# Splits of w_out, a bias and the sink on other engines and in other places, and the tile order of the output projections

## The chip, the cores and the metric

The kernel runs on one core of a Trainium2 chip. The metric is device time in microseconds (us); the profile names the engines PE (TensorE, matmul), DVE (VectorE), ACT (ScalarE), POOL (GpSimd) and SP (SyncE, which here only issues DMAs).

## The reference

A trunk of two layers over x of 1024 tokens by 1024 features, with 256 memory tokens, all float32; a final RMSNorm stands behind the second layer.

```python
# layer 0
aq, ak, av, bq, bk, bv, xq, gate = split(rmsnorm(x, norm_g) @ w_in)
y_a = windowed_gqa_sink(aq, ak, av, sink, table)   # |i-j| <= 128, bias by distance, 6 heads
y_b = dense_gqa(rope(rmsnorm(bq)), rope(rmsnorm(bk)), bv)          # 6 heads
y_x = memory_cross_attention(xq, mem_n, w_mem_kv)                  # 4 heads
x = x + (concat(y_a, y_b, y_x) * silu(gate)) @ w_out
# layer 1: 6 heads of differential attention (softmax minus lam * softmax) in the place of a and b
# in windowed_gqa_sink, for each head and query:
p = softmax(concat([logits, sink_col], axis=-1), axis=-1)[..., :-1]
```

The sink is one more logit per head, which adds to a softmax's sum and has no value row.

## The kernel before

**Numbers.** Every float32 factor of a matmul is kept as two parts, a rounded high half and the rest as a low half (names: `wh`/`wl` of input weights, `woh`/`wol` of w_out, `yh`/`yl` of the gated head outputs, `PTh`/`PTl` of the transposed probabilities). A product is three matmuls: high by high, high by low, low by high.

**Stages.** Layer 0: the normalised x and its transposes, then attention. Attention is a list of steps, one for a head and 128 queries (dense, "B", and cross-attention, "X") or a head and twice 128 queries (windowed, "A"): 8 of X, 8 of the first B head, and then 40 of B and 24 of A mixed by the pattern `PAT`. `run_steps` writes them out: the scores of step i (PE, `sb` or `sa` in a PSUM buffer of 128x1024, of which there are two), the exponential, the normalisation; a hop of the probabilities through a DMA (`er<-e`, on SP's queue); three steps later (`LAG`) their transposes on PE (`te`, `ta`) and, a step after, the product with the values (`ob`, `oa`). Between these pieces run_steps draws matmuls from a queue of jobs: the projections of heads that come later (`acc`), and when those are done the partial output projection (`pre`, L660), which multiplies the head outputs that are finished by w_out. Nothing of this order is decided at run time: each engine carries out its instructions as the program, after a scheduler, has them, and waits where an operand is missing.

**A dense step.** DVE takes the minimum `mn` of the negated scores (L1059) and multiplies it by the query's norm, `mr` (L1063, 128x1); ACT computes exp with `mr` as bias and the row sums `z` (L1064, 128x1024); DVE the reciprocal `rz` (L1067); POOL multiplies (L1068).

**A windowed step.** For each of its two query blocks DVE adds the distance bias and takes the minimum with the sink (`nsink`, its negative) in one instruction (L1132); ACT computes exp with sums (L1136, 128x384, or 128x256 at the ends of the sequence). Then ACT computes the sink's own exponential `es` (L1139, 128x2), DVE adds it to the sums (L1141) and takes the reciprocal (L1143), POOL multiplies twice (L1149).

**The splits of w_out.** `load_wout` (L248 to L258) loads a piece of 128x512 of w_out by DMA (`wor`), ACT casts it to the high half (L257), and DVE (even pieces) or POOL (odd ones) subtracts for the low half (L258). There are 16 pieces in a layer, two column halves of 8; `wout_hook` calls it from between the steps once the input projections are far enough.

**Output projection.** `out_proj` takes the 8 token tiles in the order `ORD[l]`. A tile is two accumulators of 128x512 (`po`), both halves of one of the two 128x1024 PSUM buffers (`ps_s`); the last tile alone has other buffers (`ps_a`, `ps_t`) and two evictions. `PRE` says which tiles have k-rows behind them from `pre`: in layer 0 the tiles 2 to 5 have 4 of 8 left (24 matmuls), 6 and 7 have 2 left (12), 0 and 1 all 8 (48); in layer 1 the tiles 2, 3 and 4 have 2 left, the others 8. Each tile is then added to x by DVE (L1274), squared and summed by ACT (L1275), normalised (DVE L1283, POOL L229, DVE L1295), and in layer 0 transposed on PE (`tx`, L344) with a split by ACT and DVE (L315, L316) to make layer 1's input `h`. The transposes of a tile stand behind the matmuls of the next one on PE.

Of the kernel before, what the change touches and what calls it, by code (L numbers as in the profile page):

```python
# [13 lines left out]
F32R = mybir.dt.float32r  # L14
# [4 lines left out]
P = 128  # L19
# [13 lines left out]
FAST = ("m0", "m1", "m2", "m3")  # L33
ORD = ((0, 1, 2, 3, 4, 5, 6, 7), (0, 1, 4, 2, 5, 3, 6, 7))
JORD = "xq0 m0 g6 m1 m2 g7 m3 bk bq0 bv bq1 g3 bq2 ak av aq0 g0 aq1 g4 g1 aq2 g5 g2".split()
# [120 lines left out]
def encoder_kernel(ctx, tc, A):  # L156
# [93 lines left out]
    def load_wout(l, i, pl):  # L250
        nh, k = divmod(i, 8)
        if k == 0:
            wtile.append([pl.tile([P, 8, 512], F32R, tag="h", name="wo" + c, bufs=4) for c in "hl"])
        raw = sg(M, "wor", F32) if i % 2 else wp.tile([P, 512], F32, tag="wr", name="wor", bufs=2)
        dma(raw, w_out[l][KORD[l][k], :, nh * 512:(nh + 1) * 512])
        hi, lo = (t[:, k, :] for t in wtile[nh])
        (nc.vector.tensor_copy if WHI[l] else nc.scalar.copy)(hi, raw)  # L257
        (nc.gpsimd if i % 2 else nc.vector).tensor_tensor(out=lo, in0=raw, in1=hi, op=ALU.subtract)  # L258
        return hi, lo
# [8 lines left out]

    wout, wtile, half = {}, [], [0]
    chunks = {}  # L270

# [762 lines left out]
    if True:  # L1034
        def b_step(h, qb):
# [8 lines left out]
            def s1(h=h, qb=qb, e=e):  # L1044
# [17 lines left out]
                mr = stat("mr")  # L1062
                nc.vector.tensor_tensor(out=mr, in0=mn, in1=rq[:, qb, h:h + 1], op=ALU.mult)  # L1063
                nc.scalar.activation(et, Sp, AF.Exp, bias=mr, scale=nrq[:, qb, h:h + 1], accum_out=z)  # L1064
                def finish():
                    rz = stat("rz")
                    nc.vector.reciprocal(rz, z)  # L1067
                    nc.gpsimd.tensor_tensor(out=et, in0=et, in1=rz.to_broadcast([P, 1024]), op=ALU.mult)  # L1068
                    e[0] = et
# [39 lines left out]
    if True:  # L1109
        def a_step(h, p):  # L1110
# [5 lines left out]
            def s1(h=h, p=p, e=e):  # L1116
# [5 lines left out]
                Sp = ps_s("sa").rearrange("p (j c) -> p j c", j=2)  # L1122
                et = new_e(M)[:, :768].rearrange("p (j c) -> p j c", j=2)
                mn = stat("mn2", 2)
                z = stat("z2", 2)
                for j in range(2):
                    qb = 2 * p + j
# [7 lines left out]
                                                   accum_out=mn[:, j:j + 1])  # L1135
                    nc.scalar.activation(et[:, j, c:c + n], et[:, j, c:c + n], AF.Exp,  # L1136
                                         bias=mn[:, j:j + 1], scale=-1.0, accum_out=z[:, j:j + 1])
                es = stat("es", 2)
                nc.scalar.activation(es, mn, AF.Exp, bias=sinkb[:, h:h + 1], scale=1.0)  # L1139
                def finish():  # L1140
                    nc.vector.tensor_tensor(out=z, in0=z, in1=es, op=ALU.add)  # L1141
                    rz = stat("rz2", 2)
                    nc.vector.reciprocal(rz, z)  # L1143
                    for j in range(2):
# [3 lines left out]
                        ej = et[:, j, c:c + hi - lo]  # L1148
                        nc.gpsimd.tensor_tensor(out=ej, in0=ej, in1=rz[:, j:j + 1].to_broadcast([P, hi - lo]), op=ALU.mult)  # L1149
                    e[0] = et  # L1150
# [3 lines left out]
            def hop(p=p, e=e):  # L1154
                t = M.at.tile([P, 1024], F32R, tag="er", name="er", bufs=M.cfg["er"])[:, :768]
                a, b = (P if p == 0 else 0), (768 - P if p == 3 else 768)
                ef = e[0].rearrange("p j c -> p (j c)")
# [51 lines left out]

    run_steps(steps, jobs, hooks0, lambda i: i % 4 != 3)  # L1210
    jobs.drain()
    top_stack.close()
# [3 lines left out]
    def out_proj(l, hT_next, stack):  # L1216
# [12 lines left out]

        def pieces(i):  # L1230
            if i < TT - 1:
                S2 = ps_s("po")
# [355 lines left out]
```

## Time and profile before

| | us |
|---|---|
| median of 3 runs | 1252.83 |
| lowest, highest | 1251.51, 1255.9 |
| profiled execution, its own time | 1255.58 |
| span of the profile | 1253.8 |
| PE busy | 1205.5 (96%) |
| DVE busy | 817.1 (65%) |
| ACT busy | 640.2 (51%) |
| POOL busy | 413.5 (33%) |

The span is what the profile covers of the execution. A matmul's end is modelled, so a busy PE need not be PE at its peak; the idle time is sure. In a row of a timeline or a group, what stands in brackets or behind the last bar is the idle time of that engine just before, and the instruction that ended it. "issue" is time in which the engine waited for nothing that the profile shows.

### The profile page before, as it was taken

The numbers are of one execution on the slowest core, as the hardware profiler recorded it, in microseconds if no ns is written. First come the engines' busy times: TensorE is split into PE (matmuls) and PEld (weight loads), VectorE is DVE, ScalarE is ACT, GpSimd is POOL, SyncE is SP. The second block draws the span as 40 slices with busy tenths as digits, with TensorE's granted clock in tenths as the row PEclk, the third lists the DMA queues.
The fourth block names the chain that finished last, engine by engine and source line by source line (L and its number), as shares of the span: only waits on it lengthen the run. The fifth ranks groups of instructions, "written<-read, shape, count | busy, mean of one in ns | idle before, by whom it ended". The sixth has DMA issues, their size and how long they took to land. (4 is left out here: it accounts for less than half of the span.)

```text
span 1253.8 us, 19637 instructions
## 1 busy us (share of the span) xinstructions
PE 1205.5 (96%) x6806; PEld 999.2 (80%) x6806; DVE 817.1 (65%) x1545; ACT 640.2 (51%) x1395; POOL 413.5 (33%) x390
## 2 busy tenths in 40 slices
PE   5999999999998999998999999999999999999997
PEld 4887788888887787887888778788887878877876
DVE  5547666377778788746355865766667666678444
ACT  6249654256666766533157644444444454456322
POOL 5023456266666565403122212212122131223100
PEclk9999999999999999999999999999999999999999
DMA  6654444545365575466644334243342433445363
GB/s 252 198 187 149 155 168 150 171 155 201 148 224 191 210 246 186 154 203 213 185 163 144 125 107 120 93 143 108 105 137 76 136 115 118 144 151 189 129 211 118
DMA packets 96350, 199.90 MB, mean 159 GB/s; under 512 B 11478, under 2 KB 31190, under 8 KB 96252
## 3 DMA queue, kind: packets, MB, share of 16 engines
q1 hardware_dynamic: 96252, 198.65, 47.4%
q8 instruction: 54, 0.88, 0.3%
q14 instruction: 44, 0.36, 0.1%
HBM read 79.32 MB, written 31.47 MB: 88 GB/s over the span
## 5 line engine op out<-in xcount | busy, mean ns | idle before, releaser
L297 PE MATMUL acc<-h,wh 128*128 128x512 f32 x1536 | 499.1, 399 | 7.3 <-DVE yt L624 3.1
L297 PEld LDWEIGHTS acc<-h,wh 128*128 128x128 f32 x1536 | 283.2, 188 | 73.3 <-issue 13.4
L297 PE MATMUL acc<-h,wl 128*128 128x512 f32 x768 | 304.6, 397 | 1.8 <-POOL wl L241 1.8
L241 POOL TENSOR_TENSOR wl<-wr,wh 128x512 fp32r<-128x512 f32 x96 | 124.9, 1302 | 340.0 <-DVE wh L239 125.2
L316 DVE TENSOR_TENSOR PTl<-te,PTh 128x512 fp32r<-128x512 f32 x224 | 148.2, 687 | 131.2 <-ACT PTh L315 128.4
L1440 ACT ACTIVATE e<-e,mn 128x1024 f32<-128x1024 f32 x96 | 110.2, 1149 | 130.7 <-DVE mn L1437 127.5
L297 PEld LDWEIGHTS acc<-h,wl 128*128 128x128 f32 x768 | 144.8, 189 | 35.5 <-issue 4.4
L315 ACT CAST PTh<-te 128x512 fp32r<-128x512 f32 x224 | 124.9, 591 | 30.2 <-PE te L540 24.6
L1068 POOL TENSOR_TENSOR e<-e,rz 128x1024 f32<-128x1024 f32 x48 | 91.7, 1913 | 78.1 <-DVE rz L1067 66.7
L1437 DVE CUSTOM_DVE_ANT_0 e<-sc,toep 128x1024 f32<-128x1024 f32 x96 | 113.9, 1217 | 5.3 <-PE sc L1431 5.0
L540 PEld LDWEIGHTS te<-identr,er 128*128 128x128 f32 x896 | 91.8, 143 | 21.1 <-issue 4.1
L540 PE MATMUL te<-identr,er 128*128 128x128 f32 x896 | 100.0, 246 | 7.5 <-issue 3.2
L239 DVE CAST wh<-wr 128x512 fp32r<-128x512 f32 x112 | 59.1, 530 | 43.9 <-PE acc L297 14.4
L1064 ACT ACTIVATE e<-sb,mr,nrq 128x1024 f32<-128x1024 f32 x48 | 58.0, 1208 | 48.4 <-DVE mr L1063 33.9
L1449 DVE SCALAR_TENSOR_TENSOR e<-e,mr 128x1024 f32<-128x1024 f32 x48 | 76.2, 1588 | 1.3
L1464 PE MATMUL oc<-PTh,v 128*128 128x256 f32 x384 | 74.8, 288 | 0.3 <-DVE ckl L1333 0.3
L660 PE MATMUL po<-woh,yh 128*128 128x512 f32 (+1 forms) x172 | 65.9, 383 | 1.5 <-DVE x L1274 1.5
L660 PE MATMUL po<-woh,yl 128*128 128x512 f32 (+1 forms) x172 | 65.6, 381 | 0.0
L660 PE MATMUL po<-wol,yh 128*128 128x512 f32 (+1 forms) x172 | 65.5, 381 | 0.0
L1464 PEld LDWEIGHTS oc<-PTh,v 128*128 128x128 f32 x384 | 61.5, 192 | 0.7 <-DVE ckl L1333 0.6
L1059 DVE TENSOR_REDUCE mn<-sb 128x1 f32<-128x1024 f32 x48 | 58.4, 1216 | 5.1 <-PE sb L509 4.7
L318 ACT ACTIVATE yh<-yr 128x256 fp32r<-128x256 f32 (+2 forms) x56 | 24.0, 448 | 67.3 <-DMA yr<-ysc 38.5
(199 smaller groups left out, 2247.1 us busy)
## 6 DMA issues: line engine op xcount, KB each, us to landing
er<-e SPq DMA_DIRECT2D x112, 512.0 KB, 2.9
wr<-in_w_in SPq DMA_DIRECT2D x96, 256.0 KB, 2.8
ysc<-gy SPq DMA_DIRECT2D x16, 512.0 KB, 2.9
wor<-in_w_out SPq DMA_DIRECT2D x32, 256.0 KB, 3.5
cq<-sg SPq DMA_DIRECT2D x64, 128.0 KB, 2.6
ck<-sg SPq DMA_DIRECT2D x48, 128.0 KB, 2.3
er<-e SPq DMA_DIRECT2D x12, 384.0 KB, 2.8
xpsc<-xh SPq DMA_DIRECT2D x18, 256.0 KB, 2.5
```

Of the source, the lines that this page charges most:

```text
L239: nc.vector.tensor_copy(hi, raw)
L241: (nc.vector if fast else nc.gpsimd).tensor_tensor(out=lo, in0=raw, in1=hi, op=ALU.subtract)
L297: lastmm[0] = nc.tensor.matmul(acc, a, b[:, k, c0:c0 + n], start=(i == 0), stop=(i == 23))
L315: nc.scalar.copy(hi, src)
L316: return nc.vector.tensor_tensor(out=lo, in0=src, in1=hi, op=ALU.subtract)
L540: nc.tensor.transpose(to[:, i * P:(i + 1) * P], e[0][:, k * P:(k + 1) * P], idt)
L660: lastmm[0] = nc.tensor.matmul(acc, a, b, start=(start and n == 0), stop=(stop and n == 2))
L1068: nc.gpsimd.tensor_tensor(out=et, in0=et, in1=rz.to_broadcast([P, 1024]), op=ALU.mult)
L1437: nc.vector.tensor_tensor_reduce(out=et, in0=Sp, in1=toeps[h][:, w0:w0 + 1024], scale=1.0, scalar=BIG, op0=ALU.add, op1=ALU.min, accum_out ...
L1440: nc.scalar.activation(et, et, AF.Exp, bias=mn[:, m:m + 1], scale=-1.0, accum_out=z[:, m:m + 1])
L1449: nc.vector.scalar_tensor_tensor(out=es[0], in0=es[1], scalar=c, in1=es[0], op0=ALU.mult, op1=ALU.add)
L1464: nc.tensor.matmul(acc, V[:, kt, v, :], pt[:, kt, :], start=(n == 0), stop=(n == 23))
```

## The change

Four parts.

1. *Splits of w_out in layer 0.* All 16 low halves go to POOL. Each has a fixed place in the order of its engine: the cast of a high half behind the exponential that was written last (`behind["exp"]`), the low half behind the normalisation written last (`behind["sub"]`). `issue_after` orders two instructions of an engine, and waits for nothing else. Layer 1's splits stay as they were.
2. *mr on ACT.* The product of minimum and norm is an ACT instruction (Identity with a scale), directly ahead of the exponential or with another ACT instruction between.
3. *The sink as a score column.* The windowed step's tile gets a further column behind each block's scores, into which ACT copies the negated sink; exp runs one column wider and its sum then holds the sink. `es` and the addition to z are gone. The rows of the hop are a column longer.
4. *Output projections.* The order of the tiles is (0, 1, 2, 6, 3, 7, 4, 5) in layer 0, where it was 0 to 7, and (0, 1, 5, 2, 6, 3, 4, 7) in layer 1, where it was (0, 1, 4, 2, 5, 3, 6, 7). In both the third tile takes two buffers of `ps_a`, which the projections and `pre` used, and is evicted in two halves.

The number of PE's instructions stays. DVE has 48 `mr`, 24 additions to z and 8 subtractions less, and 2 additions and the halved third tiles more; ACT has 48 `mr` and 30 copies of the sink more, and 24 `es` less; POOL has 8 subtractions more.

```diff
--- before.py
+++ after.py
@@ -31,7 +31,7 @@
 CUTS = ((0, 4, 6, 8), (0, 4, 6, 7, 8))
 LAG = 3
 FAST = ("m0", "m1", "m2", "m3")
-ORD = ((0, 1, 2, 3, 4, 5, 6, 7), (0, 1, 4, 2, 5, 3, 6, 7))
+ORD = ((0, 1, 2, 6, 3, 7, 4, 5), (0, 1, 5, 2, 6, 3, 4, 7))
 JORD = "xq0 m0 g6 m1 m2 g7 m3 bk bq0 bv bq1 g3 bq2 ak av aq0 g0 aq1 g4 g1 aq2 g5 g2".split()
 NB0 = 1
 PAT = "BBABBABBABBABBAA" * 4
@@ -254,8 +254,11 @@
         raw = sg(M, "wor", F32) if i % 2 else wp.tile([P, 512], F32, tag="wr", name="wor", bufs=2)
         dma(raw, w_out[l][KORD[l][k], :, nh * 512:(nh + 1) * 512])
         hi, lo = (t[:, k, :] for t in wtile[nh])
-        (nc.vector.tensor_copy if WHI[l] else nc.scalar.copy)(hi, raw)
-        (nc.gpsimd if i % 2 else nc.vector).tensor_tensor(out=lo, in0=raw, in1=hi, op=ALU.subtract)
+        own = l == 0 and behind["sub"] is not None
+        with (tc.issue_after(behind["exp"].ins) if own else nullcontext()):
+            (nc.vector.tensor_copy if WHI[l] else nc.scalar.copy)(hi, raw)
+        with (tc.issue_after(behind["sub"].ins) if own else nullcontext()):
+            (nc.gpsimd if own or i % 2 else nc.vector).tensor_tensor(out=lo, in0=raw, in1=hi, op=ALU.subtract)
         return hi, lo
 
     def wout_hook(l, jobs, last, pl):
@@ -267,6 +270,7 @@
                 wout[len(wout)] = load_wout(l, len(wout), pl)
 
     wout, wtile, half = {}, [], [0]
+    behind = {"exp": None, "sub": None}
     chunks = {}
 
     def half_done(n=1):
@@ -1060,12 +1064,13 @@
                 et = new_e(M)
                 z = stat("z")
                 mr = stat("mr")
-                nc.vector.tensor_tensor(out=mr, in0=mn, in1=rq[:, qb, h:h + 1], op=ALU.mult)
-                nc.scalar.activation(et, Sp, AF.Exp, bias=mr, scale=nrq[:, qb, h:h + 1], accum_out=z)
+                nc.scalar.activation(mr, mn, AF.Identity, scale=rq[:, qb, h:h + 1])
+                behind["exp"] = nc.scalar.activation(et, Sp, AF.Exp, bias=mr, scale=nrq[:, qb, h:h + 1], accum_out=z)
                 def finish():
                     rz = stat("rz")
                     nc.vector.reciprocal(rz, z)
-                    nc.gpsimd.tensor_tensor(out=et, in0=et, in1=rz.to_broadcast([P, 1024]), op=ALU.mult)
+                    behind["sub"] = nc.gpsimd.tensor_tensor(out=et, in0=et, in1=rz.to_broadcast([P, 1024]),
+                                                            op=ALU.mult)
                     e[0] = et
                 return finish
             st.s1 = s1
@@ -1120,9 +1125,15 @@
                     jobs.ensure("aq%d" % ((h + 1) // 2))
                     load_q(Aq, aq_d, h + 1)
                 Sp = ps_s("sa").rearrange("p (j c) -> p j c", j=2)
-                et = new_e(M)[:, :768].rearrange("p (j c) -> p j c", j=2)
+                et = new_e(M)[:, :770].rearrange("p (j c) -> p j c", j=2)
                 mn = stat("mn2", 2)
                 z = stat("z2", 2)
+                ends = [(min(8, qb + 2) - qb + 1) * P for qb in (2 * p, 2 * p + 1)]
+                if ends[0] == ends[1]:
+                    nc.scalar.copy(et[:, :, ends[0]], nsink[:, h:h + 1].to_broadcast([P, 2]))
+                else:
+                    for j in range(2):
+                        nc.scalar.copy(et[:, j, ends[j]:ends[j] + 1], nsink[:, h:h + 1])
                 for j in range(2):
                     qb = 2 * p + j
                     lo, hi = max(0, qb - 1) * P, min(8, qb + 2) * P
@@ -1133,12 +1144,9 @@
                                                    in1=abias[h][:, c:c + n], scale=1.0,
                                                    scalar=nsink[:, h:h + 1], op0=ALU.add, op1=ALU.min,
                                                    accum_out=mn[:, j:j + 1])
-                    nc.scalar.activation(et[:, j, c:c + n], et[:, j, c:c + n], AF.Exp,
-                                         bias=mn[:, j:j + 1], scale=-1.0, accum_out=z[:, j:j + 1])
-                es = stat("es", 2)
-                nc.scalar.activation(es, mn, AF.Exp, bias=sinkb[:, h:h + 1], scale=1.0)
+                    behind["exp"] = nc.scalar.activation(et[:, j, c:c + n + 1], et[:, j, c:c + n + 1], AF.Exp,
+                                                         bias=mn[:, j:j + 1], scale=-1.0, accum_out=z[:, j:j + 1])
                 def finish():
-                    nc.vector.tensor_tensor(out=z, in0=z, in1=es, op=ALU.add)
                     rz = stat("rz2", 2)
                     nc.vector.reciprocal(rz, z)
                     for j in range(2):
@@ -1146,14 +1154,15 @@
                         lo, hi = max(0, qb - 1) * P, min(8, qb + 2) * P
                         c = lo - (qb - 1) * P
                         ej = et[:, j, c:c + hi - lo]
-                        nc.gpsimd.tensor_tensor(out=ej, in0=ej, in1=rz[:, j:j + 1].to_broadcast([P, hi - lo]), op=ALU.mult)
+                        behind["sub"] = nc.gpsimd.tensor_tensor(
+                            out=ej, in0=ej, in1=rz[:, j:j + 1].to_broadcast([P, hi - lo]), op=ALU.mult)
                     e[0] = et
                 return finish
             st.s1 = s1
 
             def hop(p=p, e=e):
-                t = M.at.tile([P, 1024], F32R, tag="er", name="er", bufs=M.cfg["er"])[:, :768]
-                a, b = (P if p == 0 else 0), (768 - P if p == 3 else 768)
+                t = M.at.tile([P, 1024], F32R, tag="er", name="er", bufs=M.cfg["er"])[:, :770]
+                a, b = (P if p == 0 else 0), (769 - P if p == 3 else 769)
                 ef = e[0].rearrange("p j c -> p (j c)")
                 dma(t[:, a:b].bitcast(F32), ef[:, a:b])
                 e[0] = t.rearrange("p (j c) -> p j c", j=2)
@@ -1208,6 +1217,7 @@
             wout_hook(0, jobs, "g2", r1)
 
     run_steps(steps, jobs, hooks0, lambda i: i % 4 != 3)
+    behind["sub"] = None
     jobs.drain()
     top_stack.close()
     att.close()
@@ -1228,6 +1238,9 @@
             return xr
 
         def pieces(i):
+            if i == 2:
+                p = [(ps_a("po")[:, 0:512], c, 512) for c in (0, 512)]
+                return p, p
             if i < TT - 1:
                 S2 = ps_s("po")
                 return [(S2[:, 0:512], 0, 512), (S2[:, 512:1024], 512, 512)], [(S2, 0, 1024)]
```

Where the first column half of w_out is split, on ACT (`woh` is a high half, `e,z` an exponential with its sum, `PTh` and `PTa` casts of transposed probabilities, `gy` and `yt` head outputs), before:

```order
L1139 ACTIVATE es<-mn_4468,small 128x2
L425 ACTIVATE gy<-acc 128x512
L437 COPY yt<-oa 64x256
L315 CAST PTa<-ta 128x3x128
L315 CAST PTa<-ta 128x2x128
L257 CAST woh<-wor 128x512 x5
L437 COPY yt<-oa 64x256
L1064 ACTIVATE e,z<-sb,mr,nrq 128x1024
L315 CAST PTh<-te 128x4x128 x2
L257 CAST woh<-wor 128x512 x2
```

and now:

```order
L319 CAST PTa<-ta 128x2x128
L1067 ACTIVATE mr<-mn,rq 128x1
L1068 ACTIVATE e,z<-sb,mr,nrq 128x1024
L259 CAST woh<-wor 128x512
L441 COPY yt<-oa 64x256
L319 CAST PTh<-te 128x4x128 x2
L259 CAST woh<-wor 128x512
L1067 ACTIVATE mr<-mn,rq 128x1
L1068 ACTIVATE e,z<-sb,mr,nrq 128x1024
L259 CAST woh<-wor 128x512
```

Before, five casts stand in a row ahead of an exponential and two behind its neighbours; now one or two stand behind each exponential, and `mr` ahead of it.

On POOL, where the first and the second column half are split (`wol` is a low half, L1068 and L1149 the normalisations), before:

```order
L1149 TENSOR_TENSOR e<-e,rz_4517 128x384
L439 TENSOR_TENSOR gy<-yt,gy 64x256
L258 TENSOR_TENSOR wol<-wor,woh 128x512 x3
L439 TENSOR_TENSOR gy<-yt,gy 64x256
L1068 TENSOR_TENSOR e<-e,rz 128x1024
L258 TENSOR_TENSOR wol<-wor,woh 128x512
L1068 TENSOR_TENSOR e<-e,rz 128x1024
L1149 TENSOR_TENSOR e<-e,rz_4701 128x384 x2
L439 TENSOR_TENSOR gy<-yt,gy 64x256
```

and now, a few steps later in the program, where most subtractions come together (lines have moved by 3 to 8: L261 was L258, L1072 was L1068, L1157 was L1149, L443 was L439):

```order
L1072 TENSOR_TENSOR e<-e,rz 128x1024
L261 TENSOR_TENSOR wol<-wor,woh 128x512
L443 TENSOR_TENSOR gy<-yt,gy 64x256
L261 TENSOR_TENSOR wol<-wor,woh 128x512
L1072 TENSOR_TENSOR e<-e,rz 128x1024
L261 TENSOR_TENSOR wol<-wor,woh 128x512 x3
L1157 TENSOR_TENSOR e<-e,rz_5049 128x384
L1157 TENSOR_TENSOR e<-e,rz_5049 128x256
L443 TENSOR_TENSOR gy<-yt,gy 64x256
L1072 TENSOR_TENSOR e<-e,rz 128x1024
L261 TENSOR_TENSOR wol<-wor,woh 128x512 x2
```

Before, POOL has three subtractions together, with none between the two dense normalisations behind them but one; now one to three stand behind nearly every normalisation.

## The prediction

> **What bounds the kernel now.** The page's first table and its chain of waits put PE ahead of all other engines, so a change is worth what it takes out of PE's idle time, or puts in.
>
> ```profile
> span 1253.8 us, 19637 instructions
> PE 1205.5 (96%) x6806; PEld 999.2 (80%) x6806; DVE 817.1 (65%) x1545; ACT 640.2 (51%) x1395; POOL 413.5 (33%) x390
> PE 39%; DVE 2%; issue 2%; ACT 1%; DMA 1%; POOL 0%; POOLq 0%; DVEq 0%; ACTq 0%
> ```
>
> PE is idle for 1253.8 - 1205.5 = 48.3 us. The view of stretches says where. Its columns are the stretch, its length, then busy us and instructions of each engine, and PE's granted clock.
>
> ```profile
> 220.00:375.00 155.00, 153.69 (x922) 131.93 (x921) 103.87 (x234) 87.63 (x191) 87.53 (x77) 1.00 0.53 180
> 375.00:530.00 155.00, 145.57 (x903) 123.13 (x901) 123.24 (x269) 103.66 (x233) 88.47 (x83) 0.99 0.56 199
> 550.00:605.00 55.00, 50.97 (x254) 41.42 (x253) 36.02 (x55) 20.99 (x42) 13.19 (x16) 1.00 0.69 215
> 1200.00:1254.00 54.00, 45.84 (x223) 38.17 (x221) 26.51 (x46) 15.50 (x35) 5.08 (x8) 0.97 0.48 163
> ```
>
> The two first are attention of layer 0, equally long. Without the splits of w_out PE idles 155 - 153.69 = 1.3 us; from 375 on, where the splits and the partial output projections (pre) stand, 155 - 145.57 = 9.4 us. DVE rises from 67% to 80% there, POOL only from 56% to 57%. The third stretch is layer 0's output projection (4.0 us idle), the fourth layer 1's, whose last idle stretch is the kernel's end. PE's waits in the second stretch:
>
> ```profile
> PE te L540 <- issue: 3.2, 5, 1.4
> PE sa L509 <- ACT e L1064: 2.1, 2, 1.1
> PE sa L509 <- DVE mn L1132: 1.3, 2, 1.1
> PE pre L660 <- DVE yt L438: 1.2, 1, 1.2
> ```
>
> The columns are total us, times, longest. What stands behind them is read in the timelines of the four engines (start, duration, engine, operation, idle time before and its releaser):
>
> ```profile
> 393.68 3.78 POOL L258 TENSOR_TENSOR wol<-wor,woh 128x512 fp32r<-128x512 f32 x3
> 394.38 3.64 DVE L258 TENSOR_TENSOR wol<-wor,woh 128x512 fp32r<-128x512 f32 x1
> 397.94 0.15 DVE L1063 TENSOR_TENSOR mr<-mn,rq 128x1 f32<-128x1 f32 x1
> 398.12 1.21 ACT L1064 ACTIVATE e<-sb,mr,nrq 128x1024 f32<-128x1024 f32 x1 [2.48 <-DVE mr L1063]
> 399.47 0.44 PE L509 MATMUL sa<-ak,q 128*128 128x384 f32 x1 [0.98 <-ACT e L1064]
> 401.43 0.50 PE L540 MATMUL te<-identr,er 128*128 128x128 f32 x4 [1.35 <-issue]
> 401.64 1.27 POOL L258 TENSOR_TENSOR wol<-wor,woh 128x512 fp32r<-128x512 f32 x1
> 401.85 1.08 DVE L1063 TENSOR_TENSOR mr<-mn,rq 128x1 f32<-128x1 f32 x1
> 405.35 0.44 PE L509 MATMUL sa<-ak,q 128*128 128x384 f32 x1 [1.07 <-DVE mn L1132]
> 427.01 0.62 ACT L257 CAST woh<-wor 128x512 fp32r<-128x512 f32 x1 [3.38 <-DMA wor<-in_w_out]
> 428.88 0.44 PE L509 MATMUL sa<-ak,q 128*128 128x384 f32 x1 [1.08 <-ACT e L1064]
> 430.65 0.50 PE L660 MATMUL pre<-woh,yh 128*128 128x512 f32 x1 [1.16 <-DVE yt L438]
> ```
>
> Read it as two chains. At 394.38 DVE begins a low half while POOL runs three of them, and is done only as POOL is; mr, the exponential's bias, is queued behind it, ACT stands 2.48 us, and PE waits three times: 0.98 + 1.35 + 1.07 = 3.40 us. At 427.01 ACT's cast of a high half had stood 3.38 us for its load, with the next exponential behind it: 1.08 + 1.16 = 2.24 us on PE. Together 5.64 of the 9.4 us.
>
> **The change, part by part.** Durations of what moves (groups of the whole run: count, busy us, mean ns; or count and min/median/max):
>
> ```profile
> L258 DVE TENSOR_TENSOR wol<-wor,woh 128x512 fp32r<-128x512 f32 x16 | 14.7, 918 | 3.5 <-ACT woh L257 3.5
> L258 POOL TENSOR_TENSOR wol<-wor,woh x8: 1274/1291/1297, 393.7 to 442.5; 128x512 fp32r<-128x512 f32 x8
> L1063 DVE TENSOR_TENSOR mr<-mn,rq 128x1 f32<-128x1 f32 x48 | 9.3, 193 | 0.7
> L1141 DVE TENSOR_TENSOR z<-z,es x24: 148/161/1109, 252.9 to 520.6; 128x2 f32<-128x2 f32 x24
> L1139 ACT ACTIVATE es<-mn,small x24: 278/280/292, 252.5 to 520.3; 128x2 f32<-128x2 f32 x24
> L1483 ACT ACTIVATE z<-ssqc,es 128x1 f32<-128x1 f32 x48 | 10.0, 258 | 4.5 <-PE ssqc L1479 4.3
> ```
>
> *Bias and sink, outside the splits.* The 48 mr leave DVE (9.3 us) for ACT, which ran none; the nearest row is another 128x1 ACTIVATE with a pointer operand, 258 ns, so ACT gets 12.4 us. The 24 es (280 ns, 6.7 us) and the 24 additions to z (161 ns) go; 30 copies of the sink into a score column come. ACT's copies of such a size are not in the trace; between nothing and the 280 ns of es they cost 0 to 8.4 us, and I take 200 ns (nearest: 258, less a pointer), 6.0 us, so they pay for es. The copies wait for no score, so they may run early. In 220 to 375 PE idles only 1.3 us: what could be gained there is at most that, and with ACT at 57% in this stretch what is added has 67 us of ACT idle to go into. A step's exponential starts 258 - 154 = 0.1 us later on its chain, which LAG (three steps between scores and transposes) covers; if that cover were gone, 48 x 0.1 = 5 us at most. I take 0, ends -1.3 and +1.7 (a third of those 5).
>
> *The splits.* Eight low halves leave DVE, at 0.69 (an undisturbed one) to 3.64 us each, and eight come to POOL at 1.29 each: +10.3 us on POOL's 88.5, 64% of the stretch. Each now stands behind a normalisation and so cannot be issued three deep ahead of a step's own; each high half stands behind the exponential that it stood ahead of. The first chain (3.40 us) rests on a DVE subtraction and a DVE mr that are both no longer there; the second (2.24) on a cast ahead of an exponential. Both go: -5.6. The remaining 3.8 us are small waits that I leave. The half clock that followed the second chain
>
> ```profile
> 431.20:434.60 3.40, 3.40 (x15) 2.80 (x14) 2.87 (x7) 2.59 (x6) 1.76 (x2) 0.50 0.69 233
> ```
>
> cost 3.40 x 0.5 = 1.7 us; no row says whether it returns after another stall, so I take half, -0.85. The low bound is all of the excess and the clock: 8.1 + 1.7 = 9.8 us. What waits on POOL's new work is the next normalisation, then its hop through DMA, then te; the hop's row (transfers, KB, median us from issue to landing):
>
> ```profile
> er<-e SPq DMA_DIRECT2D x112, 512.0 KB, 2.9
> ```
>
> These 2.9 us must still fit after a later normalisation. I take +0.5, ends 0 and the 10.3 us of rival 1. Sum of this part: -6.
>
> The Trainium skill speaks on the first chain in SBUF — State Buffer, section "Who interferes with whom": a DVE instruction with two SBUF inputs blocks against a GpSimd instruction that reads SBUF, each for the other's whole length. The 3.64 and the 1.08 us rows agree, and by that rule more subtractions on POOL block whatever such DVE work is left; that would take up to 10.3 us from DVE's relief. On the half clock, TensorE: Matmul & The Clock Gate ("What's actually happening") has a free-running window of 3413 ns that lowers the clock after an idle window; the 3.40 us row has its length, and by the rule the whole 1.7 us returns with the stall, 0.85 less than my sum.
>
> *Output projection of layer 0.* PE's four waits there:
>
> ```profile
> PE tx L344 <- DVE h L316: 1.7, 1, 1.7
> PE tx L344 <- DVE xs L1295: 1.2, 2, 0.7
> PE acc L297 <- DVE v L1283: 1.1, 1, 1.1
> ```
>
> The tiles 6 and 7 (12 matmuls left, against 24 of the tiles 2 to 5) move between longer ones. That gives the last tiles more matmuls to hide a normalisation under (the 1.1 and part of the 1.7 should go, about -2.3), but behind a short tile the transposes of the one before come early. One matmul of this kind takes the distance between two starts:
>
> ```profile
> 1200.17 0.39 PE L660 MATMUL po<-wol,yh 128*128 128x512 f32 x1
> 1200.40 0.39 PE L660 MATMUL po<-woh,yl 128*128 128x512 f32 x1
> ```
>
> so 12 fewer are 12 x 0.23 = 2.8 us less cover. I work out two new waits of about 0.9, so -0.5; ends -4.0 (all waits go) and +3.2 (both new ones as long as the longest here, 1.7, and nothing saved but 0.2).
>
> *Layer 1's end.* The third tile now takes two other PSUM buffers and need not wait for tile 0's to be emptied:
>
> ```profile
> PE po L660 <- DVE x L1274: 1.5, 1, 1.5
> ```
>
> -1.5; ends -1.5 and 0 (the other buffers not free either: they last held partial sums finished well before). The work after the last matmul stays.
>
> **Sum**, against the profiled execution: 0 - 6 - 0.5 - 1.5 = -8.0 us. That execution took 1255.6 us (span 1253.8), 2.7 above the median 1252.8 of the three runs and at their upper end, which no row explains; I carry the difference over to the median: **1244.8, say 1245 us**. All low ends give -1.3 - 9.8 - 4.0 - 1.5 = -16.6, 1236 us.
>
> **Rivals.**
> 1. *POOL becomes the late engine* (slower). Three subtractions still stand in a row in one place and two in another, 1.29 us each, ahead of a step's normalisation. If each of the eight added ones delays its step's te by its whole length, PE idles 8 x 1.29 = 10.3 us more, and by the blocking seen at 401.85 (1.08 us for a 0.15 us instruction) DVE's own work pays too, so that the chains' 5.6 do not come back: +10.3 - 0.5 - 1.5 = +8.3, 1261 us. It decides from the point where more than half of a subtraction shows on PE. For it: te waits already head the list of PE's waits (3.2 us). Against: POOL has 155 - 88.5 = 66.5 us idle in this stretch.
> 2. *Nothing gained among the splits.* ACT, 67% busy there, gets mr, copies and waits at mr for the maximum as it did at the exponential; or the small waits take the place of the long ones. Then the tail and projection alone: -2.0, 1250.8. For it: the waits are spread over five tiles and five releasers. Against: the two chains' owners are taken away outright.
> 3. *The short tiles expose the transposes*: +3.2 in the place of -0.5, 1244.8 + 3.7 = 1248.5. For it: DVE's xs and h are the releasers of every wait there.
> 4. *The fixed places make w_out late*: the last low half stands about one step later, and a partial projection must wait for it. The price is a step, counted by the dense steps' normalisations in this stretch:
>
> ```profile
> L1068 POOL TENSOR_TENSOR e<-e,rz x20: 1887/1893/2266, 383.3 to 512.4; 128x1024 f32<-128x1024 f32 x20
> ```
>
> With half as many windowed steps beside these 20, a step is 130 / 30 = 4.3 us: 1249.1. Against: no PE wait for wol is in the list of waits, so there is room.
>
> **How the numbers follow.** Forecast 0.62 (its own range 1239 to 1249); rival 1 0.12; rival 2 0.13; rival 3 0.08; rival 4 0.05. Faster or slower by over 0.3% (3.8 us, about what this measurement can tell) means below 1249.0 or above 1256.6. The forecast is faster, with half of rival 3 and a few hundredths of the rest: 0.68; the same has rivals 2 and 4 and the other half of 3, 0.20; slower is rival 1, 0.12. The range 1237 to 1255 leaves out rival 1 and the last of the low side.
>
> **What would show it.** In the stretch of the splits PE's idle time falls from 9.4 to about 4 us; no DVE instruction there lasts over 2 us; no exponential stands 2 us for mr or behind a cast; DVE falls to some 110 us, POOL rises to near 99. PE's clock in that stretch tells the half-clock term. In 550 to 605 idle time stays near 4 us with other tiles' names in it; in the tail "po <- DVE x" is gone. I am wrong if te's waits grow and end on POOL's normalisations (rival 1), if PE's idle time among the splits stays above 8 us (rival 2), if tx waits sum to over 6 us (rival 3), or if pre waits for wol (rival 4).

## The result and the profile after

The changed kernel took 1246.9 us (median of 6 runs, 1245.4 to 1247.6) against 1254.4 for the kernel before (6 runs): ratio 0.9938, 95% interval 0.9924 to 0.9953, or 7.8 us less. Timed again later beside other kernels, it was 1249.3 against 1253.4: ratio 0.9961 (0.9948 to 0.9974), 4.9 us less. So it is faster, by 5 to 8 us. Part of the distance between the two timings is PE's granted clock, whose mean was 0.9973 in the first and 0.9953 in the second. Compared within its kernel, over the 160 runs of these experiments, a run was 0.56 us longer for each us that its clock withheld (one minus the clock, times the span). By that estimate the clock makes some 1.4 of the 2.4 us between the timings; where it matters below, differences are also given with the clock taken out in this way.

The page of the kernel after, its span and first table:

```profile
span 1245.0 us, 19673 instructions
PE 1201.2 (96%) x6806; PEld 998.5 (80%) x6806; DVE 801.6 (64%) x1471; ACT 652.1 (52%) x1453; POOL 422.1 (34%) x398
```

PE is still the bound. DVE lost 15.5 us, ACT gained 11.9 and POOL 8.6. The same four stretches as in the prediction, of the kernel after (the last reaches 9 us beyond its end):

```profile
220.00:375.00 155.00, 154.41 (x942) 134.04 (x941) 105.12 (x212) 94.05 (x222) 92.57 (x83) 1.00 0.54 187
375.00:530.00 155.00, 145.13 (x901) 123.56 (x900) 109.00 (x223) 106.13 (x249) 96.73 (x88) 0.99 0.55 197
550.00:605.00 55.00, 52.29 (x257) 42.50 (x256) 36.35 (x59) 20.10 (x41) 12.71 (x15) 1.00 0.71 224
1200.00:1254.00 54.00, 38.75 (x194) 32.89 (x192) 23.12 (x42) 12.28 (x32) 4.24 (x8) 0.96 0.42 148
```

The surprise stands in the second row. DVE fell from 123 to 109 us there, as predicted, and PE is idle for 155 - 145.13 = 9.9 us, where it was 9.4. PE's waits in that stretch:

```profile
PE oa L1196 <- ACT PTa L319: 2.0, 1, 2.0
PE te L544 <- issue: 2.0, 3, 1.5
PE sa L513 <- DVE mn L1143: 2.0, 2, 1.1
PE te L544 <- PE sa L513: 1.5, 2, 0.8
PE sa L513 <- ACT e L1068: 0.9, 1, 0.9
```

Behind the longest of them stands a chain like the prediction's second: a cast of a high half waits for its load, an exponential and the cast PTa stand behind it, and PE waits for PTa (ACT, then PE):

```profile
431.11 0.62 ACT L259 CAST woh<-wor 128x512 fp32r<-128x512 f32 x1 [2.17 <-DMA wor<-in_w_out]
431.64 0.51 ACT L1147 ACTIVATE e<-e,mn 128x257 f32<-128x257 f32 x1
433.16 0.86 ACT L319 CAST PTa<-ta 128x384 fp32r<-128x384 f32 x2
434.07 0.39 PE L1196 MATMUL oa<-PTa,av 128*128 128x256 f32 x1 [2.05 <-ACT PTa L319]
```

Stretches of fixed time hold other work once something ahead moves. So the traces are compared at places of the program: the first dense scores of layer 0, the 48th of the 96 windowed-score matmuls (about where the splits begin), the first matmul of the output projection, the first and last scores of layer 1, the end. Each number is the change of a piece's length against the kernel before, in us of one profiled execution; under "cut windows" stands how often PE's clock was halved for 3.4 us (1.7 us each), ahead of the first dense scores and among the splits.

| kernel | to first scores | attention, no splits | splits | projection, start of layer 1 | layer 1 | end | cut windows |
|---|---|---|---|---|---|---|---|
| before (length) | 142.1 | 234.1 | 154.5 | 158.7 | 470.5 | 93.9 | 1, 1 |
| after | -2.1 | -2.8 | -1.1 | -1.0 | +0.4 | -2.2 | 0, 1 |
| after, again | -2.1 | -3.0 | -0.6 | -0.8 | -0.6 | -2.2 | 0, 1 |
| splits alone | -0.7 | -0.1 | +4.7 | -0.8 | -1.6 | 0.0 | 1, 1 |
| mr alone | -2.3 | -1.8 | -1.0 | -0.2 | +0.6 | 0.0 | 0, 1 |
| sink alone | -2.6 | -0.5 | +0.1 | 0.0 | -0.2 | 0.0 | 0, 0 |
| projections alone | -0.6 | -0.1 | -0.6 | -0.3 | +1.0 | -2.2 | 1, 1 |
| all but splits | -0.6 | -2.9 | +0.9 | -1.5 | 0.0 | -2.2 | 1, 2 |
| all but mr | -2.2 | -0.4 | +2.4 | -1.9 | -0.2 | -2.3 | 0, 2 |
| all but sink | -2.3 | -1.8 | -1.5 | -0.5 | -1.1 | -2.3 | 0, 2 |
| mr on DVE, scalar form | -0.6 | -1.3 | -2.5 | -0.9 | -0.1 | -2.2 | 1, 0 |
| even low halves on DVE | -0.5 | -3.0 | +0.7 | -1.1 | -0.1 | -2.2 | 1, 2 |
| own buffer | -0.9 | -2.8 | +0.8 | -1.4 | -0.5 | -2.2 | 1, 3 |
| own buffer, cast moved | -1.9 | -2.9 | -0.2 | -1.3 | -0.1 | -2.2 | 0, 2 |

The column "to first scores" is no gain of the change: it falls into two groups that go with the cut windows there, and the kernel with the projections alone, whose program is still the one before at that place, and the kernel before differ by 0.6 in it. The columns "projection" and "layer 1" scatter by over 1 us among kernels that are the same there. What the change brings lies in the columns "attention, no splits" and "end". The column "splits" has to be read with the cut windows among the splits: without the splits part it shows +0.9 with two windows, and less the 1.7 us of the second one -0.8, which is what the whole change shows with one (-1.1 and -0.6).

### The profile page after: what moved, and what is told of

Its sections match the earlier page's. It is cut to its first block, busy times and chain, and to the rows that moved or that the text cites. A ratio compares the mean times of both kernels' runs of the same rounds, so it can differ in the third digit from the quotient of the medians.

```text
span 1245.0 us, 19673 instructions
## 1 busy us (share of the span) xinstructions
PE 1201.2 (96%) x6806; PEld 998.5 (80%) x6806; DVE 801.6 (64%) x1471; ACT 652.1 (52%) x1453; POOL 422.1 (34%) x398
## 5 line engine op out<-in xcount | busy, mean ns | idle before, releaser
L1072 POOL TENSOR_TENSOR e<-e,rz 128x1024 f32<-128x1024 f32 x48 | 91.1, 1901 | 77.1 <-DVE rz L1071 58.0
L1068 ACT ACTIVATE e<-sb,mr,nrq 128x1024 f32<-128x1024 f32 x48 | 57.9, 1207 | 2.1
```

The source lines that it names most:

```text
L1072: behind["sub"] = nc.gpsimd.tensor_tensor(out=et, in0=et, in1=rz.to_broadcast([P, 1024]), op=ALU.mult)
```

## The experiments

Four kernels hold one part each, three lack one part each, one puts mr on DVE in another form, and three alter the splits of the changed kernel. Each was timed in 5 to 12 executions.

### Each part alone

**Splits alone** (fixed places, all low halves of layer 0 on POOL):

```diff
-        (nc.gpsimd if i % 2 else nc.vector).tensor_tensor(out=lo, in0=raw, in1=hi, op=ALU.subtract)
+        with (tc.issue_after(behind["sub"].ins) if own else nullcontext()):
+            (nc.gpsimd if own or i % 2 else nc.vector).tensor_tensor(out=lo, in0=raw, in1=hi, op=ALU.subtract)
...
```

> Only the splits of w_out in layer 0 are changed (all low halves on POOL, both halves in fixed places). Theory 1, the prediction's sum: this part is worth most, -6 us against the kernel before, and PE's idle time among the splits falls from 9.4 to about 4 us. Theory 2, from the trace after (PE idles 9.9 us there, the long waits have come back in other places: a cast of a high half that waits 2.17 us for its load, a yh cast that waits 2.86 us, both ahead of an exponential): this part is worth -1 us at most, 0 within what can be told.

Measured: 1257.1 us, ratio 1.0028 (1.0017 to 1.0039), 3.5 us slower. Neither theory had this. Two rows of its timelines (POOL, then DVE) show it:

```profile
448.22 1.90 POOL L1072 TENSOR_TENSOR e<-e,rz 128x1024 f32<-128x1024 f32 x1
448.28 1.85 DVE L1145 TENSOR_TENSOR z<-z,es 128x2 f32<-128x2 f32 x1
```

and the instructions of two lines in it (min/median/max):

```profile
L1067 DVE TENSOR_TENSOR mr<-mn,rq x48: 141/159/1368, 143.8 to 514.0; 128x1 f32<-128x1 f32 x48
L1145 DVE TENSOR_TENSOR z<-z,es x24: 148/163/1848, 252.1 to 524.5; 128x2 f32<-128x2 f32 x24
```

An addition of 128x2 that takes 0.16 us otherwise took 1.85, and ended as POOL's normalisation did. mr took up to 1.37. Not one mr or addition that began while POOL was idle took over 0.17 us, here or in the kernel before; the long ones all began while POOL was at work, and some that did were short all the same. More work on POOL means that such an instruction meets it more often: 12 of the 48 mr began under POOL here, and 6 before.

**mr alone** on ACT:

```diff
-                nc.vector.tensor_tensor(out=mr, in0=mn, in1=rq[:, qb, h:h + 1], op=ALU.mult)
+                nc.scalar.activation(mr, mn, AF.Identity, scale=rq[:, qb, h:h + 1])
```

> Only mr (128x1) moves from DVE to ACT. Theory 1, the sum: 0 (-1.3 to +1.7). Theory 2, from the two traces, where the change gains 2.8 us between the first dense scores and the first partial output projection's stretch, of which mr and the sink column are the only parts: -2 us, and DVE's relief shows in all of layer 0's attention, where 40 steps lose a DVE instruction that stood between the minimum and the exponential.

Measured: 1250.1 us, ratio 0.9975 (0.9964 to 0.9986), 3.1 us faster. Theory 2 had the sign and about the size: 1.8 us of it lie in the attention ahead of the splits, where PE had 1.3 us of plain idle time in the stretch from 220 to 375.

**Sink column alone**:

```diff
-                es = stat("es", 2)
-                nc.scalar.activation(es, mn, AF.Exp, bias=sinkb[:, h:h + 1], scale=1.0)
...
-                    nc.vector.tensor_tensor(out=z, in0=z, in1=es, op=ALU.add)
+                nc.scalar.copy(et[:, :, ends[0]], nsink[:, h:h + 1].to_broadcast([P, 2]))
...
```

> Only the sink becomes a score column (es on ACT and the addition on DVE go, copies on ACT come). Theory 1: 0. Theory 2: a windowed step loses a DVE instruction and a wait between ACT and DVE ahead of its reciprocal, -1 us over 24 steps; if mr brings the whole 2.8 us of the attention before the splits, 0.

Measured: 1255.0 us, ratio 1.0007 (0.9994 to 1.0019): no difference that can be told. The marks give -0.5 us ahead of the splits.

**Output projections alone**:

```diff
-ORD = ((0, 1, 2, 3, 4, 5, 6, 7), (0, 1, 4, 2, 5, 3, 6, 7))
+ORD = ((0, 1, 2, 6, 3, 7, 4, 5), (0, 1, 5, 2, 6, 3, 4, 7))
...
+            if i == 2:
+                p = [(ps_a("po")[:, 0:512], c, 512) for c in (0, 512)]
+                return p, p
```

> Only the output projections change (order of the tiles, third tile in two other buffers). Theory 1, the sum: -0.5 in layer 0 and -1.5 in layer 1, together -2. Theory 2, from the two traces: the marks of PE gain 1.0 us between the first po of layer 0 and the first scores of layer 1, and 2.2 us from the last scores of layer 1 to the end: -3.2. This run also shows whether the 2.1 us that the trace after is ahead by at the first dense scores, where the two programs do not yet differ, comes and goes by itself: its program is the one before up to the output projection.

Measured: 1251.8 us, ratio 0.9985 (0.9974 to 0.9995), 1.9 us faster, -2 expected by the one and -3.2 by the other. The end gains 2.2 to 2.3 us in every kernel that has this part, and 0.0 in the three that lack it; layer 0's projection changes by -0.3 here. (The +1.0 in layer 1 of this run holds a cut window at 722 us, worth 1.7.)

The four ratios add to 3.5 - 3.1 + 0.9 - 1.9 = -0.6 us, each sure to some 1.4 us. The whole gives -4.9 to -7.8. The parts hang together.

### One part taken from the whole

Theory L says why: a DVE instruction that reads two tensors from SBUF can stand still while POOL works, and mr, the addition to z and the even low halves are such instructions. Its rival M: the splits do not matter, the sum fails between mr and the sink column.

**All but the splits:**

```diff
-        own = l == 0 and behind["sub"] is not None
-        with (tc.issue_after(behind["exp"].ins) if own else nullcontext()):
...
+        (nc.gpsimd if i % 2 else nc.vector).tensor_tensor(out=lo, in0=raw, in1=hi, op=ALU.subtract)
```

> The whole change but the splits (mr on ACT, sink column, output projections). The four parts alone gave +3.5, -3.1, +0.9 and -1.9 us by their ratios, which add to -0.6, where the whole gives -7.8. Theory L: a DVE instruction with two SBUF inputs stands still while POOL works; subtractions on POOL hurt only while mr and the addition to z are on DVE, and with both gone they bring the prediction's gain. Then this kernel is near the sum of the other three, -4 us (1250), 3 to 4 us slower than the whole change. Theory M: what does not add is mr with the sink column, and the splits are worth nothing: this kernel is as fast as the whole change (1246 to 1247).

Measured: 1248.8, ratio 0.9973 (0.9959 to 0.9987), 3.4 us faster than before, which is L's -4. Against the whole it is 1.5 us slower by the second timing of the whole (0.9961) and 4.4 by the first (0.9938); with the second the intervals overlap. With the clock taken out this kernel is 5.4 us faster than the one before, and the whole in its second timing 5.7. So a gain from the splits in this company is not shown, and M's price for them, nothing, stands. That they no longer cost 3.5 us is shown. M's reason falls: mr, sink column and projections alone add to -4.1 us, near the -3.4 of the three together, so it is the splits that do not add.

**All but mr** (mr on DVE, as before):

```diff
-                nc.scalar.activation(mr, mn, AF.Identity, scale=rq[:, qb, h:h + 1])
+                nc.vector.tensor_tensor(out=mr, in0=mn, in1=rq[:, qb, h:h + 1], op=ALU.mult)
```

> The whole change but mr, which is back on DVE. Theory L: mr is blocked by the 16 subtractions and the normalisations on POOL (in the splits alone its mean was 359 ns, against 240 before and about 150 undisturbed), so most of the gain is lost: 1252 to 1255. Theory M: the splits do not matter, and mr's own 3.1 us are lost: about 1250.

Measured: 1251.4, ratio 0.9991 (0.9980 to 1.0002). Of the gain 3.8 (second timing) to 6.6 us (first) are lost; the time lies between L's range (1252 to 1255) and M's 1250.

**All but the sink column:**

```diff
-                    behind["exp"] = nc.scalar.activation(et[:, j, c:c + n + 1], et[:, j, c:c + n + 1], AF.Exp,
+                    behind["exp"] = nc.scalar.activation(et[:, j, c:c + n], et[:, j, c:c + n], AF.Exp,
...
+                    nc.vector.tensor_tensor(out=z, in0=z, in1=es, op=ALU.add)
```

> The whole change but the sink column: es and the addition to z are back. Theory L: the addition (two SBUF inputs, 483 ns mean among the splits alone, against 246 before) is blocked, with the minimum of the next windowed block behind it: 2 to 3 us slower than the whole change, about 1249.5. Theory M or any in which only mr matters: as fast as the whole change, since the sink column alone gave nothing.

Measured: 1246.7, ratio 0.9960 (0.9946 to 0.9974): that of the whole's second timing, and 2.8 us slower than its first. L's price of 2 to 3 us is not shown, though the longest addition took 2.15 us in this kernel. The other three parts alone add to -1.5 us here, and to +2.5 without mr, where -5.0 and -1.1 were measured. By these sums, sure to some 2.5 us, either mr or the addition off DVE takes most of the splits' cost away. Why one is enough stays open.

**mr on DVE with one tensor input**, and otherwise the whole change:

```diff
-                nc.scalar.activation(mr, mn, AF.Identity, scale=rq[:, qb, h:h + 1])
+                nc.vector.tensor_scalar(out=mr, in0=mn, scalar1=rq[:, qb, h:h + 1], scalar2=None, op0=ALU.mult)
```

> The whole change, but mr is on DVE in a form with one tensor from SBUF and a 128x1 scalar operand. Theory L: an instruction of one SBUF stream is not blocked (the 128x1 reciprocals, which read one, took 160 ns in every run), so mr takes 150 to 200 ns and the time is that of the whole change, 1246 to 1247, or a little better, as ACT loses 48 instructions of 300 ns. Theory Q: what costs is any DVE instruction between the minimum and the exponential, whatever its inputs, since it queues behind other work: as slow as with mr back on DVE (1250 to 1255).

Measured: 1248.2, ratio 0.9962 (0.9949 to 0.9975): as fast as the second timing of the whole, with mr on ACT, and 3.6 us faster than with mr on DVE as a product of two tensors, with intervals that do not meet. With the clock taken out 2.2 of the 3.6 us are left. Both kernels have mr on the same engine, between the same instructions; only the operand's form differs. All 48 mr of the two kernels (first the two-tensor form):

```profile
L1067 DVE TENSOR_TENSOR mr<-mn,rq x48: 140/159/1364, 142.3 to 510.3; 128x1 f32<-128x1 f32 x48
```

```profile
L1067 DVE TENSOR_SCALAR mr<-mn,rq x48: 189/211/217, 143.9 to 505.8; 128x1 f32<-128x1 f32 x48
```

The scalar form is slower at its median and never over 217 ns, though 14 of the 48 began while POOL was at work; of the two-tensor form 13 did, and 10 of those took over 200 ns. So theory Q, that any DVE instruction in this place costs as much as the two-tensor one, falls. Whether the scalar form gives all that ACT gives is open: in the attention ahead of the splits the marks show -1.3 us with it, -0.4 with the two-tensor form and -2.8 to -3.0 with mr on ACT.

The Trainium skill has the rule, in SBUF — State Buffer, section "Who interferes with whom": a DVE instruction with two SBUF inputs contends with a GpSimd instruction that reads SBUF, and the loser blocks. These rows agree. The page counts `tensor_scalar` among the operations that can contend as well, under conditions; at 128x1 float32 with a 128x1 scalar none of the 48 did.

### What is left among the splits

**Even low halves back on DVE**, odd ones on POOL in their places:

```diff
-        with (tc.issue_after(behind["sub"].ins) if own else nullcontext()):
-            (nc.gpsimd if own or i % 2 else nc.vector).tensor_tensor(out=lo, in0=raw, in1=hi, op=ALU.subtract)
+        with (tc.issue_after(behind["sub"].ins) if own and i % 2 else nullcontext()):
+            (nc.gpsimd if i % 2 else nc.vector).tensor_tensor(out=lo, in0=raw, in1=hi, op=ALU.subtract)
```

> The whole change, but the even pieces' low halves stay on DVE (without a place), the odd ones on POOL behind a normalisation; the high halves keep their places. Theory P, the prediction's first chain: a subtraction on DVE stands still while POOL works (3.64 and 3.98 us rows) and the exponential's minimum or the transposes queue behind it, so the gain that the splits bring in company of the other parts (about 4 us) is lost: 1250. Theory Q: what the splits bring is their places behind the exponentials and normalisations; half of the subtractions on DVE changes nothing: as fast as the whole change.

 

Measured: 1249.5, ratio 0.9967 (0.9956 to 0.9979), beside **the whole again** on the same chip:

> The changed kernel once more, on the same chip as the three runs beside it, as what they are compared with: 0.994 of the kernel before, as measured. If its ratio is nearer 0.996, the runs that lacked one part (0.9960 without the sink column, 0.9962 with mr as a scalar form on DVE) cost nothing against it.

Measured: 1249.3, ratio 0.9961 (0.9948 to 0.9974). So it lay nearer 0.996, and the two are the same: theory P's 4 us are not there, and where the even low halves are done decides nothing that can be told once mr and the sink are off DVE's two-tensor list. Among the even low halves that stayed on DVE the longest took 2.18 us, not 3.6.

**A buffer of its own for the even pieces of w_out.** In the kernel after, these are PE's two longest waits from 405 to 410, with what stood ahead of them on SP, ACT and POOL:

```profile
400.98 1.29 POOL L261 TENSOR_TENSOR wol<-wor,woh 128x512 fp32r<-128x512 f32 x1
402.29 0.38 SPq L175 DMA_DIRECT2D yr<-ysc  x1
405.19 0.63 ACT L322 ACTIVATE yh<-yr 128x512 fp32r<-128x512 f32 x1 [2.86 <-DMA yr<-ysc]
405.73 1.19 ACT L1068 ACTIVATE e<-sb,mr,nrq 128x1024 f32<-128x1024 f32 x1
407.06 0.44 PE L513 MATMUL sa<-ak,q 128*128 128x384 f32 x1 [0.94 <-ACT e L1068]
409.60 0.72 PE L544 MATMUL te<-identr,er 128*128 128x128 f32 x4 [1.46 <-issue]
```

The subtraction ends at 402.27, and its raw buffer is one of the two that `yr` is loaded into; the load starts at 402.29, ACT's cast waits for it, the exponential stands behind the cast, and PE waits 0.94 us for that. That the 1.46 us hang on the same chain is not shown.

```diff
-        raw = sg(M, "wor", F32) if i % 2 else wp.tile([P, 512], F32, tag="wr", name="wor", bufs=2)
+        raw = (sg(M, "wor", F32) if i % 2 else M.pl.tile([P, 512], F32, tag="wor", name="wor", bufs=1) if l == 0
+               else wp.tile([P, 512], F32, tag="wr", name="wor", bufs=2))
```

> The whole change, and in layer 0 the even pieces of w_out are loaded into a buffer of their own, no longer into the two that the loads of yr use. In the changed kernel a load of yr started at 402.29, as a subtraction on POOL ended (402.27); ACT's yh waited for it 2.86 us with an exponential behind it, and PE 0.94 + 1.46 us. Theory R, the buffer holds up yr: these 2.4 us go, about -2 us against the whole change. Theory S: the wait moves to the load of w_out itself, which now has one buffer for every second piece: 0.

Measured: 1247.9, ratio 0.9956 (0.9943 to 0.9969): the whole, within its interval. ACT's waits for yr among the splits fell from 6.6 us (the whole, again) to 0.9, so the buffer was the cause of that wait; but no gain in time can be told. POOL, DVE, PE in this kernel:

```profile
395.72 1.29 POOL L262 TENSOR_TENSOR wol<-wor,woh 128x512 fp32r<-128x512 f32 x1
396.98 1.88 POOL L1073 TENSOR_TENSOR e<-e,rz 128x1024 f32<-128x1024 f32 x1
398.83 2.48 POOL L262 TENSOR_TENSOR wol<-wor,woh 128x512 fp32r<-128x512 f32 x2
396.33 5.53 DVE L324 SCALAR_TENSOR_TENSOR yl<-yr,yh 128x512 fp32r<-128x512 f32 x1
401.78 1.28 DVE L321 TENSOR_TENSOR PTl<-te,PTh 128x512 fp32r<-128x512 f32 x2
402.51 0.58 PE L1087 MATMUL ob<-PTl,v 128*128 128x256 f32 x1 [4.36 <-DVE PTl L321]
```

yh came early, its low half yl (two tensors from SBUF) began while POOL was at work, and stood through four of POOL's instructions in a row, 5.53 us for 0.69; PTl was behind it on DVE, and PE waited 4.36. PE's clock was at half for 6.8 us from 400.7, two cut windows in a row; 5.0 us of them came after the wait and withheld some 2.5 us of PE's work. One of the 2 us rows there (the columns as in the stretches above, PE's clock behind POOL's count):

```profile
404.00:406.00 2.00, 2.00 (x12) 2.00 (x11) 0.36 (x2) 0.84 (x3) 1.34 (x2) 0.50 0.06 16
```

The profile of the kernel after has one such window among the splits, this one three.

**The same, with the cast behind the second block's exponential:**

```diff
-                    behind["exp"] = nc.scalar.activation(et[:, j, c:c + n + 1], et[:, j, c:c + n + 1], AF.Exp,
+                    x = nc.scalar.activation(et[:, j, c:c + n + 1], et[:, j, c:c + n + 1], AF.Exp,
...
+                behind["exp"] = x
```

> As the run with a buffer of their own, and a high half that falls in a windowed step stands behind the exponential of the second block, no longer between the two. In the changed kernel such a cast waited 2.17 us for its load with the second exponential behind it, and PE 2.05 us. If that chain is what is left of the splits' cost: another -2 us, 1243 in all. If the cast then only delays the next instruction, the cast of the transposed probabilities: no gain over the run with the buffer alone.

Measured: 1248.8, ratio 0.9963 (0.9951 to 0.9975): no gain over the buffer alone, as its second theory had it. PE's wait for the cast probabilities (`oa <- PTa`) stayed at 1.8 us, and the 4.4 us wait stood in this kernel too. No kernel tried here is shown to beat the changed one.

## Why the prediction was right, and where it was not

The sum, -8.0 us and 1245, met the first timing (-7.8, 1246.9), and the direction holds in both. Its terms did not: the largest of them brought nothing that can be told, and what was gained came in good part from a piece that the sum took at 0. That the total came out near is luck. By the prediction's own sign rival 2 is what happened among the splits: PE idles 9.9 us there, over its limit of 8, with other waits in the place of the two chains.

1. **"The splits: Both go: -5.6."** The failing step. The chain from the 3.64 us subtraction did go: no DVE subtraction is left. The one of a cast that waits for its load went at 427, and one like it came at 431 (rows above), with 2.05 us on PE where it was 2.24. Among the splits the marks show -1.1 and -0.6 us, and PE's waits there are as long as before, under other names. The step took a stall's removal for its price. It did not ask what stands behind the same POOL train next: yl on DVE, a load of yr whose buffer a subtraction holds, a cast behind its own load. By itself this part costs 3.5 us; taken out of the whole it is not missed by any amount that can be told. (The blocked subtraction was also read as done when POOL was; by the rows it ended 0.56 us after the last of POOL's three, close to the 0.69 that it takes undisturbed.)
2. **"Bias and sink, outside the splits: I take 0."** Measured -2.8 and -3.0 in that piece, beyond the low end of -1.3. The step bounded the gain by PE's plain idle time in the stretch from 220 to 375; but the piece is longer (142 to 376, 2.1 us idle before and 1.1 after), and 1.8 of the 2.8 us lie in time that the profile calls busy: the same 1347 matmuls take 232.1 us of it before and 230.3 after, at full clock both times. Why they follow one another faster is not shown; PE's idle time was no upper bound. With mr alone the piece gains 1.8 us, with the sink column alone 0.5. And the step priced mr at its duration, where it was a two-tensor instruction among POOL's work. As costs the estimates were near: mr on ACT 295 ns (258 taken), a copy of the sink some 205 (200 taken):

```profile
L1067 ACT ACTIVATE mr<-mn,rq x48: 277/295/307, 142.4 to 503.9; 128x1 f32<-128x1 f32 x48
L1133 ACT COPY e<-nsink x18: 181/207/221, 248.2 to 506.2; 128x2 f32<-128x2 f32 x18
```

3. **"Output projection of layer 0: -0.5."** -0.3 to -1.9 by the marks, with a scatter of over 1 us among kernels that are the same there. The projection stands 6 us earlier in the kernel after, so the fixed stretch does not show the same work; moved by as much (544 to 599), PE's four waits of 4.0 us have become five of 3.2, all of them tx for xs:

```profile
PE tx L348 <- DVE xs L1308: 3.2, 5, 1.2
```

So the waits for h (1.7) and v (1.1) went, as forecast, shorter ones came, and -0.8 stands against the -0.5.

4. **"Layer 1's end: -1.5."** Right in its mechanism, and -2.2 or -2.3 in size in all runs with this part: the wait is gone, and PE idles 1.7 us less from layer 1's last scores to the end. The other 0.5 lies in time that the profile calls busy; it is not accounted for.
5. **The half clock, "-0.85".** Nothing: one cut window stands among the splits in the kernel after as before. The whole profile has one less, but ahead of the change.
6. **Rival 1** had the mechanism that mattered in its second half, the blocking of DVE's own work, and its sign: the splits alone are slower, though by 3.5 us and not by the 10.3 that it put on them. In the whole it did not decide: with mr or the addition to z off DVE most of that cost is gone by the sums above. The prediction used the blocking as what POOL's new work could cost, and did not ask what it is worth to take mr out of its way, though it quoted mr's 1.08 us row.

## What to carry to other kernels

A short two-tensor instruction on VectorE that sits between a reduction and an exponential can cost what GpSimd happens to be doing, not its median; look at the longest of its line beside POOL's timeline, and give it one tensor and a scalar operand, or another engine, before GpSimd gets more work. Parts of a change that touch one such conflict are not additive: one that loses alone can cost nothing in company. A wait taken out of a stage that is full on three engines is worth only what the next wait leaves.

## What the hardware showed

- **A blocked DVE instruction can stand through several POOL instructions in a row**: 5.53 us through four of them without a gap (rows above), and before the change 3.64 us through three. It does not always: with the splits alone an mr ended at 444.84, as the first of three subtractions did (444.83), with the next ones right behind (POOL, then DVE). What decides between the two is not shown.

```profile
443.54 3.78 POOL L261 TENSOR_TENSOR wol<-wor,woh 128x512 fp32r<-128x512 f32 x3
444.38 0.46 DVE L1067 TENSOR_TENSOR mr<-mn,rq 128x1 f32<-128x1 f32 x1
```

- **The same PE stall may or may not halve the clock.** Every profile has a stall of about 1.8 us near 129 us. Rows of 2 us each of the kernel before, and then of the kernel after (PE's clock is the number behind POOL's count):

```profile
132.00:134.00 2.00, 2.00 (x6) 1.54 (x5) 1.97 (x4) 2.00 (x9) 0.73 (x1) 0.50 0.27 103
```

```profile
132.00:134.00 2.00, 2.00 (x11) 1.65 (x9) 1.88 (x4) 1.79 (x8) 0.55 (x1) 1.00 0.34 131
```

In 7 of 14 profiled executions 3.4 us at half clock follow, and in 7 none, with the same instructions up to there or nearly so. It is worth 1.7 us (the two groups lie 1.6 us apart at the first dense scores), more than several of the effects looked for here, so that two single profiles should not be compared by their spans alone.
